# Gate weights of a retrieval layer: stored by 64 tokens instead of 32, with one-hot matrices built for 8 tokens at a time instead of 16

## The chip, the cores and the metric

The kernel runs on one core of a Trainium2 chip. The metric is the device time of one execution in microseconds. Before the change it is 2794.61 us, the median of 3 runs (2793.46 to 2800.45).

## The reference, cut to what matters

One layer of a trunk over 1024 tokens of width 1024, all in float32. An attention and a recurrent branch come first and play no part in the change. Then comes a retrieval layer (PEER) with 16384 experts; an expert is one neuron, a row of `expert_down` and a row of `expert_up`:

```python
v1, i1 = lax.top_k(s1, 16); v2, i2 = lax.top_k(s2, 16)      # per token, 8 heads
sc, ci = lax.top_k(v1[..., :, None] + v2[..., None, :], 16) # 16 of the 256 sums
eid = i1[ci // 16] * 128 + i2[ci % 16];  g = softmax(sc)    # 8 x 16 = 128 experts a token
act = gelu(einsum('thkd,td->thk', expert_down[eid], xb))
out = einsum('thk,thkd->td', g * act, expert_up[eid])
```

The output is the final RMSNorm of the residual plus this.

## The kernel before, in words

The 1024 tokens are 8 blocks of 128. The retrieval is done in two ways at once. For the first 3 blocks (NG) the kernel **gathers**: for each of 128 slots an indirect DMA on GpSimd's queue (L831) brings one 4 KB row for each of 128 tokens into one of 5 `row` buffers, and VectorE multiplies it (L848 for the down rows, L858 to add an up row into `accg`). That is 768 gathers. They are paced by `gather_steps(n)`, which is called from the loops of the other work; each VectorE step of a gather is pinned behind the VectorE instruction that was written just before it.

For the other 5 blocks (ND, 640 tokens, TD) the kernel is **dense**. The experts are 128 groups e of 128 neurons. For each e, `down_all` (L980) loads 512 KB of `down_t`, splits it into a high and a low part (ScalarE `dh`, VectorE `dl`) and runs 48 matmuls of 320 columns; the GELU of that is `ga`. It is weighted by a dense matrix of gates: for each token, a 128 x 128 matrix that is zero but in its 128 chosen places.

These gate matrices are made in the **one-hot stage** (L1078 to L1133). For TB tokens at a time, `one_hots` makes `o` (one-hot rows of both key indices, VectorE L1089, 3 buffers), `ov` (one of them times the gate's high and middle part, VectorE L1093, 2 buffers) and `oa` (times its low part, ScalarE, one instruction a token, L1100, 2 buffers). `weights` then runs 3 matmuls a token (L1113) into PSUM, 4 tokens to a bank, and ScalarE copies each bank into `st`, [128, 128 groups, TG tokens] (L1116, 2 buffers). When `st` has its TG tokens, two DMAs on ScalarE's queue store it to `gw_d` in HBM (L1118 the first 32 groups, L1119 the other 96). Each pass of the loop makes the one-hots of its own TB tokens, then, as its share comes due, a `down_all` whose result is kept in HBM (`act`; 40 of the 128 in this stage, one for each 16 tokens), then the matmuls of the TB tokens before, then its share of 168 gathers (none in the last 96 tokens). `turn` (L1126) transposes the top-k results of the last block at token 32.

In the **up stage** (L1138 on) `weigh(e)` reads, for every 4 groups e, `gw` (1280 KB, 2 buffers; L1151) from `gw_d`, takes `ga` from HBM (L1157) or from `down_all`, multiplies (L1162) and splits it into `w_h` and `w_l`. Then 15 matmuls of 512 columns for each e and half of the width add it to the output. `uraw` (L1189) are the rows of `expert_up`. Gathers run along here too. At the very end come those that are left and the final norm.

SyncE's queue (SP) issues `draw`, `uraw`, `acc`, `gw` and `ga` in order; ScalarE's queue issues `act` and the stores of `gw_d`; GpSimd's the gathers. The order of each engine's and queue's instructions is fixed at compile time by a planner, which takes the program's order as priority and moves an instruction up or down by its own estimate of when operands, buffers and transfers are ready; pinned instructions stay behind their predecessor. Memory on chip is a stack of pools: `sl`, `oh` and `stage` (which holds `st`) lie where `acc`, `up`, `wp` and `gp` (which holds `gw`) come later, so a new tile can wait for the last reader of an old one. The tile addresses of this kernel put the first `gw` buffer over the second `st` buffer.

The lines that make the stored layout and its read:

```python
gw_d = [dram.tile([TD // TG, P, n, TG], F32, name="gw_d") for n in (E_FIRST, NK - E_FIRST)]
gws[e // EQ] = gw = gp.tile([P, TD // TG, EQ * TG], F32, name="gw")
nc.sync.dma_start(gw, part[:, :, k:k + EQ, :].rearrange("a p e t -> p a (e t)"))
```

Of the kernel before, what the change touches and what calls it, by code (L numbers as in the profile page):

```python
# [43 lines left out]
EG = 8  # L44
EQ = 4
EARLY = 4
TG = 32
TB = 16
TI = 2

G_ATT, G_OUT, G_QRY, G_TOPK, G_OH = 45, 30, 30, 0, 168
# [1 line left out]
B_OUT, B_CHAIN, B_TURN, B_QRY, B_TOPK = 0, 3, 8, 8, 12  # L53
A_STEPS, A_AHEAD, A_FILL, LRU_AT, WO_AT = 3, 4, 0.5, 0.7, 50
E_QRY, E_TOPK, E_OH = 8, 20, 40
TURN5 = 2
OH_LAST = 96
NORM_IN = ((0,), (1,), (2, 3))
NORM_B = ((0, 1), (2, 3))
# [42 lines left out]
def trunk(  # L102
# [825 lines left out]
    with tc.tile_pool(name="op_d", bufs=1) as op, \  # L928
            tc.tile_pool(name="ps_od", bufs=3, space=PSUM) as ps_a:
        def turn(i, xt):  # L930
            for q in range(2):
                pt = ps_t.tile([P, 4, P], F32, name="pt")
                for j in range(4):
                    t = T.transpose(pt[:, j, :], xt[:, (4 * q + j) * P:(4 * q + j + 1) * P], ident)
                    if j == 0:
                        tc.keep_in_program_order(t)
                for j in range(4):
                    sl = (slice(None), 4 * q + j, slice(i * P, (i + 1) * P))
                    g2 = g2c[:, 4 * q + j:4 * q + j + 1]
                    A.activation(xH[sl], pt[:, j, :], AF.Copy, scale=g2)  # L940
                    V.scalar_tensor_tensor(xL[sl], pt[:, j, :], g2, xH[sl].bitcast(F32),
                                           op0=ALU.mult, op1=ALU.subtract)
# [31 lines left out]
    act_d = {}  # L974
    gw_d = [dram.tile([TD // TG, P, n, TG], F32, name="gw_d") for n in (E_FIRST, NK - E_FIRST)]

# [29 lines left out]
    with ExitStack() as ph:  # L1006
# [68 lines left out]
        V.tensor_copy(key_t, key_f[:, :, None].broadcast_to([P, P, TI]))  # L1075
        GB = TB // TI

        def one_hots(t0):  # L1078


            b, tt = divmod(t0, P)
            g0 = tt // TI

            def per_slot(t, n):
                return t[:, g0:g0 + GB, :, None, :].broadcast_to([P, GB, n, P, TI]).rearrange(
                    "p g n k i -> p (g n) k i")

            o = oh.tile([P, GB, 2, P, TI], BF, name="o21", bufs=3)
            V.tensor_tensor(o.rearrange("p g n k i -> p (g n) k i"),  # L1089
                            key_t[:, None, :, :].broadcast_to([P, GB * 2, P, TI]),  # L1090
                            per_slot(slot_k[b], 2), op=ALU.is_equal)
            ov = oh.tile([P, GB, 2, P, TI], BF, name="o1v", bufs=OB)
            V.tensor_tensor(ov.rearrange("p g n k i -> p g n (k i)"),  # L1093
                            o[:, :, 1:2, :, :].rearrange("p g n k i -> p g n (k i)").broadcast_to(
                                [P, GB, 2, P * TI]),
                            per_slot(slot_w[b], 2), op=ALU.mult)
            oa = oh.tile([P, GB, P, TI], BF, name="o1a", bufs=OB)
            for t in range(TB):
                g, j = divmod(t, TI)
                A.activation(oa[:, g, :, j], o[:, g, 1, :, j], AF.Copy,  # L1100
                             scale=slot_a[b][:, tt + t:tt + t + 1])
            return o, (ov[:, :, 0], ov[:, :, 1], oa)

        def weights(t0, o, parts):
            if t0 % TG == 0:
                sts[t0 // TG] = st_pool.tile([P, NK, TG], F32, name="st")
            st = sts[t0 // TG]
            for t4 in range(0, TB, 4):
                ps = ps_g.tile([P, 4, P], F32, name="pg")
                for t in range(t4, t4 + 4):  # L1110
                    g, j = divmod(t, TI)
                    for i, part in enumerate(parts):
                        T.matmul(ps[:, t - t4, :], o[:, g, 0, :, j], part[:, g, :, j],  # L1113
                                 start=i == 0, stop=i == 2)
                c = t0 % TG + t4
                A.copy(st[:, :, c:c + 4], ps.rearrange("p t i -> p i t"))  # L1116
            if (t0 + TB) % TG == 0:
                nc.scalar.dma_start(gw_d[0][t0 // TG], st[:, :E_FIRST, :])  # L1118
                nc.scalar.dma_start(gw_d[1][t0 // TG], st[:, E_FIRST:, :])  # L1119

        sts = {}
        last_five, last = last, None
        for t0 in range(0, TD, TB):
            now = one_hots(t0)
            if t0 == TURN5 * TB:
                turn(*last_five)  # L1126
# [153 lines left out]
```

## Time and profile before

| | us |
|---|---|
| median of 3 runs | 2794.61 |
| the profiled execution, its own time | 2791.39 |
| its span, first to last instruction | 2789.4 |
| TensorE (PE) busy | 2621.7 (94% of the span) |
| VectorE (DVE) busy | 2291.3 (82%) |
| ScalarE (ACT) busy | 1218.7 (44%) |
| GpSimd (POOL) busy | 1092.4 (39%) |

The profile counts 770 MB moved, 276 GB/s over the span. "PEclk" or "granted clock" is the share of TensorE's full clock (2.4 GHz) that it was given; 0.5 is 1.2 GHz. "DMA share" is the mean busy share of the 16 DMA engines. PEld is TensorE's weight load, SPq and ACTq are DMA issues of those queues. Of an instruction's row, the bracket says how long its engine stood idle before it and what ended that.

### The profile page before, as it was taken

Reading aid. Unit: us, or ns where it says so; the run is one execution under the profiler, and the core shown is the slowest. Engines: PE = TensorE matmul, PEld = TensorE weight load, DVE = VectorE, ACT = ScalarE, POOL = GpSimd, SP = SyncE. Lnnn points to the kernel's source line nnn. Section 1 sums busy time; section 2 is a strip of 40 time slices with the busy share of each in tenths; the row PEclk is TensorE's granted clock in tenths of the full one; section 3 lists DMA queues with packets and bytes.
Section 4 is the critical chain, followed back from the end, with each engine's and each line's share of the span. In section 5 each row is a group of like instructions: output and inputs, shape, how many; then the busy total and the mean of one; then the engine's idle time right before and its main releaser. Section 6 shows DMA issues by size and latency. Waiting matters only on the chain.

```text
span 2789.4 us, 43339 instructions
## 1 busy us (share of the span) xinstructions
PE 2621.7 (94%) x15489; PEld 2304.8 (83%) x15489; DVE 2291.3 (82%) x4838; ACT 1218.7 (44%) x2598; POOL 1092.4 (39%) x906
## 2 busy tenths in 40 slices
PE   7989988898999999999989999999999999999991
PEld 5765966647998999999978888888888888888871
DVE  7553879977999988989958888888888888888887
ACT  5652437824334667888833222222222222222220
POOL 2210035451111035444334445555455445545564
PEclk9999989999999999999999999999999999999996
DMA  6655489775544369999999999999999999999997
GB/s 199 144 139 174 119 196 235 227 276 182 181 142 132 111 234 336 347 344 340 331 364 336 340 325 345 348 323 340 338 339 336 320 344 340 339 327 341 333 316 257
DMA packets 316520, 770.05 MB, mean 276 GB/s; under 512 B 25632, under 2 KB 126000, under 8 KB 313744
## 3 DMA queue, kind: packets, MB, share of 16 engines
q0 software_dynamic: 136432, 425.67, 45.8%
q1 hardware_dynamic: 162768, 274.37, 29.2%
q10 hardware_dynamic: 17104, 67.25, 6.1%
q8 instruction: 121, 1.98, 0.3%
q14 instruction: 95, 0.78, 0.1%
HBM read 681.86 MB, written 85.33 MB: 275 GB/s over the span
## 4 chain that ended last, share of the span: by engine, by line
PE 75%; issue 9%; DMA 8%; DVE 4%; ACT 2%; POOL 2%; SPq 0%; DVEq 0%; POOLq 0%; ACTq 0%
PE pu L144 10%; PE pu L147 9%; PE pu L148 9%; PE pd L144 8%; PE pd L148 8%; PE pd L147 8%; PE pg L1113 4%; PE pa L144 2%; PE pa L148 2%; PE pa L147 2%; DMA row<-in_expert_up,eid 2%; PE pp L144 2%; PE pp L147 2%; PE pp L148 2%; DMA row<-in_expert_down,eid 2%
## 5 line engine op out<-in xcount | busy, mean ns | idle before, releaser
L831 POOL DMA_INDIRECT row<-in_expert_down,eid x384 | 507.8, 1322 | 660.0 <-DVE row L848 515.4
L831 POOL DMA_INDIRECT row<-in_expert_up,eid x384 | 505.0, 1315 | 587.2 <-DVE accg L858 403.5
L144 PE MATMUL pd<-xdH,dh 128*128 128x320 f32 x2048 | 639.8, 313 | 4.7 <-ACT dh L124 4.0
L148 PE MATMUL pd<-xdH,dl 128*128 128x320 f32 x2048 | 630.2, 312 | 13.4 <-DVE dl L125 13.3
L147 PE MATMUL pd<-xdL,dh 128*128 128x320 f32 x2048 | 635.2, 311 | 0.0
L858 DVE SCALAR_TENSOR_TENSOR accg<-row,wg,accg 128x1024 f32<-128x1024 f32 x384 | 491.4, 1280 | 23.8 <-DMA row<-in_expert_up,eid 21.3
L147 PE MATMUL pu<-ul,w_h 128*128 128x512 f32 x1280 | 501.9, 392 | 1.0 <-DVE ul L125 1.0
L148 PE MATMUL pu<-uh,w_l 128*128 128x512 f32 x1280 | 498.4, 391 | 0.0
L848 DVE SCALAR_TENSOR_TENSOR row<-row,x2g 128x1024 f32<-128x1024 f32 x384 | 462.5, 1219 | 23.2 <-DMA row<-in_expert_down,eid 22.5
L144 PE MATMUL pu<-uh,w_h 128*128 128x512 f32 x1280 | 393.9, 393 | 11.7 <-issue 5.2
L148 PEld LDWEIGHTS pd<-xdH,dl 128*128 128x128 f32 x2048 | 385.7, 189 | 21.6 <-DVE dl L125 15.5
L144 PEld LDWEIGHTS pd<-xdH,dh 128*128 128x128 f32 x2048 | 387.7, 189 | 12.9 <-ACT dh L124 4.3
L147 PEld LDWEIGHTS pd<-xdL,dh 128*128 128x128 f32 x2048 | 387.6, 189 | 7.5
L124 ACT CAST uh<-uraw 128x512 fp32r<-128x512 f32 x256 | 157.6, 620 | 472.3 <-PE pu L148 385.0
L144 PEld LDWEIGHTS pu<-uh,w_h 128*128 128x128 f32 x1280 | 236.7, 188 | 55.5 <-issue 7.3
L147 PEld LDWEIGHTS pu<-ul,w_h 128*128 128x128 f32 x1280 | 241.1, 188 | 48.7 <-DVE ul L125 1.8
L148 PEld LDWEIGHTS pu<-uh,w_l 128*128 128x128 f32 x1280 | 240.3, 188 | 48.4
L124 ACT CAST dh<-draw 128x512 fp32r<-128x512 f32 x256 | 158.0, 619 | 231.3 <-PE pd L147 225.8
L125 DVE TENSOR_TENSOR dl<-draw,dh 128x512 fp32r<-128x512 f32 x256 | 175.1, 687 | 74.5 <-ACT dh L124 74.0
L125 DVE TENSOR_TENSOR ul<-uraw,uh 128x512 fp32r<-128x512 f32 x256 | 175.5, 687 | 65.3 <-ACT uh L124 64.9
L124 ACT CAST w_h<-ga 128x640 fp32r<-128x640 f32 x128 | 93.2, 729 | 245.2 <-PE pu L147 148.8
L1100 ACT ACTIVATE o1a<-o,slot_a 128x128 bf16<-128x128 bf16 x640 | 194.7, 430 | 0.6 <-issue 0.3
(265 smaller groups left out, 4089.5 us busy)
## 6 DMA issues: line engine op xcount, KB each, us to landing
draw<-in_down_t SPq DMA_DIRECT2D x128, 512.0 KB, 7.0
uraw<-in_up_h SPq DMA_DIRECT2D x128, 512.0 KB, 6.8
gw<-gw_d SPq DMA_DIRECT2D x32, 1280.0 KB, 16.4
gw_d<-st ACTq DMA_DIRECT2D x20, 1536.0 KB, 11.5
act<-ga ACTq DMA_DIRECT2D x70, 320.0 KB, 4.8
ga<-act SPq DMA_DIRECT2D x70, 320.0 KB, 9.8
wraw<-in_w_query SPq DMA_DIRECT2D x64, 256.0 KB, 3.1
gw_d<-st ACTq DMA_DIRECT2D x20, 512.0 KB, 7.4
```

The lines of the kernel that those rows point to most:

```text
L124: A.copy(hi, src)
L125: (eng or V).tensor_sub(lo, src, hi.bitcast(F32))
L144: t = T.matmul(ps, wh, mh, start=first, stop=False)
L147: T.matmul(ps, wh, ml, start=False, stop=False)
L148: T.matmul(ps, wl, mh, start=False, stop=last)
L831: nc.gpsimd.indirect_dma_start(out=r, out_offset=None, in_=table, in_offset=bass.IndirectOffsetOnAxis(ap=eids[tb][:, s:s + 1], axis=0))
L848: tc.keep_in_program_order(V.scalar_tensor_tensor(r, r, 1.0, x2, op0=ALU.mult, op1=ALU.mult, accum_out=act[:, s:s + 1]))
L858: tc.keep_in_program_order(V.scalar_tensor_tensor(acc, r, w[:, s:s + 1], acc, op0=ALU.mult, op1=ALU.add))
L1100: A.activation(oa[:, g, :, j], o[:, g, 1, :, j], AF.Copy, scale=slot_a[b][:, tt + t:tt + t + 1])
L1113: T.matmul(ps[:, t - t4, :], o[:, g, 0, :, j], part[:, g, :, j], start=i == 0, stop=i == 2)
```

## The change

Three constants. TG is the number of tokens that one `st` tile and one slab of `gw_d` hold; TB the number of tokens for which one call of `one_hots` and of `weights` works; TURN5 counts in units of TB and keeps `turn` at token 32.

```diff
-TG = 32
-TB = 16
+TG = 64
+TB = 8
 TI = 2
...
-TURN5 = 2
+TURN5 = 4
```

By the code above this means: `one_hots` is called 80 times instead of 40, each VectorE instruction in it has half the elements; the buffers of `o`, `ov` and `oa` keep their number and have half the size; a `down_all` comes in every second pass of the loop; a call of `gather_steps` hands out half as many gathers, twice as often; `st` is twice as large and is stored 10 times, with twice the bytes each time; a `gw` read has the same bytes in contiguous runs of 4 x 64 x 4 bytes = 1 KB instead of 512 B.

## Rows read from the trace of the kernel before

**Rows 1.** Stretches of the span: us, busy of each engine (instructions), clock, DMA share, GB/s

```profile
1300.00:1406.00 106.00, 106.00 (x1071) 104.88 (x1070) 92.97 (x72) 93.35 (x252) 41.24 (x31) 1.00 0.92 341
1406.00:1427.00 21.00, 20.67 (x141) 20.40 (x140) 11.41 (x12) 5.91 (x13) 7.07 (x6) 1.00 1.02 418
1427.00:1460.00 33.00, 21.77 (x101) 19.56 (x102) 15.42 (x17) 6.05 (x11) 7.39 (x7) 0.79 0.98 344
1500.00:1600.00 100.00, 100.00 (x528) 88.77 (x527) 80.96 (x133) 28.64 (x49) 40.99 (x35) 1.00 0.94 335
2733.00:2789.00 56.00, 0.17 (x1) 0.00 (x0) 42.34 (x101) 1.87 (x4) 25.34 (x20) 0.53 0.72 257
```

**Rows 2.** Waits of TensorE, 956 to 1406 us: us in total, times, longest

```profile
PE pd L148 <- DVE dl L125: 5.4, 2, 5.1
```

**Rows 3.** Groups by shape, 956 to 1406 us: busy us, mean ns | idle before

```profile
L1093 DVE TENSOR_TENSOR o1v<-o,slot_w 128x4096 bf16<-128x4096 bf16 x38 | 87.0, 2289 | 6.3 <-PE pg L1113 6.2
L1089 DVE TENSOR_TENSOR o<-key_t,slot_k 128x4096 bf16<-128x4096 bf16 x37 | 84.5, 2284 | 3.1 <-PE pg L1113 3.1
L665 DVE TENSOR_TENSOR wt<-ge,dx 128x2048 bf16<-128x2048 bf16 x5 | 6.1, 1218 | 0.1
```

**Rows 4.** VectorE in order of time, one pass of the one-hot loop: start, us

```profile
1382.99 2.30 DVE L1093 TENSOR_TENSOR o1v<-o,slot_w 128x4096 bf16<-128x4096 bf16 x1 [0.29 <-PE pg L1113]
1385.21 2.28 DVE L1089 TENSOR_TENSOR o<-key_t,slot_k 128x4096 bf16<-128x4096 bf16 x1
1387.42 1.27 DVE L858 SCALAR_TENSOR_TENSOR accg<-row,wg,accg 128x1024 f32<-128x1024 f32 x1
1388.87 0.69 DVE L125 TENSOR_TENSOR dl<-draw,dh 128x512 fp32r<-128x512 f32 x1 [0.18 <-ACT dh L124]
...
1392.86 2.30 DVE L1093 TENSOR_TENSOR o1v<-o,slot_w 128x4096 bf16<-128x4096 bf16 x1 [0.29 <-PE pg L1113]
```

**Rows 5.** The chain of waits in order of time: the gate matmuls of two passes: start, us

```profile
1350.67 2.77 PE pg L1113 x48
1360.53 2.77 PE pg L1113 x48
```

**Rows 6.** DMA issues, whole span: count, KB each, median us to landing

```profile
draw<-in_down_t SPq DMA_DIRECT2D x128, 512.0 KB, 7.0
gw<-gw_d SPq DMA_DIRECT2D x32, 1280.0 KB, 16.4
gw_d<-st ACTq DMA_DIRECT2D x20, 1536.0 KB, 11.5
```

**Rows 7.** Issue queues of ScalarE and SyncE at the handover to the up stage: start, us

```profile
1406.51 0.76 ACTq L1119 DMA_DIRECT2D gw_d<-st  x1
...
1427.27 14.21 SPq L1151 DMA_DIRECT2D gw<-gw_d  x2
1441.57 6.34 SPq L985 DMA_DIRECT2D draw<-in_down_t  x1
1447.95 0.91 SPq L1157 DMA_DIRECT2D ga<-act  x2
```

**Rows 8.** VectorE at the handover: start, us, [idle before]

```profile
1447.33 0.83 DVE L1162 TENSOR_TENSOR ga<-ga,gw 128x640 f32<-128x640 f32 x1 [4.65 <-DMA gw<-gw_d]
1455.07 0.83 DVE L1162 TENSOR_TENSOR ga<-ga,gw 128x640 f32<-128x640 f32 x1 [4.10 <-DMA ga<-act]
1458.34 0.82 DVE L1162 TENSOR_TENSOR ga<-ga,gw 128x640 f32<-128x640 f32 x1
```

**Rows 9.** Waits from 1406 us to the end: us in total, times, longest

```profile
DVE ga L1162 <- DMA ga<-act: 53.5, 13, 5.9
DVE accg L858 <- DMA row<-in_expert_up,eid: 18.7, 24, 2.6
```

**Rows 10.** Gathers issued after 2733 us, and VectorE's last of them

```profile
L831 POOL DMA_INDIRECT row<-in_expert_up,eid x20: 937/1208/1918, 2732.1 to 2765.0; - x20
2769.42 2.69 DVE L858 SCALAR_TENSOR_TENSOR accg<-row,wg,accg 128x1024 f32<-128x1024 f32 x2 [0.74 <-DMA row<-in_expert_up,eid]
```

## The prediction

> **What bounds the kernel now.** I read the stretches of the span first [rows 1]. From 1300 to 1406 us, at the end of the one-hot stage, TensorE is busy the whole time at full clock, while VectorE is busy 88% (92.97 of 106), ScalarE 88% and the DMA engines 92%. So TensorE sets the pace there, with three resources close behind it. In the list of its waits from 956 to 1406 us TensorE has one entry, 5.4 us [rows 2]: the one-hots never keep it waiting. From 1500 us TensorE is again busy without a break (100.00 of 100), and what it does there the change does not touch. Two stretches are not TensorE's. The first is the handover, 1406 to 1460 us. There the DMA engines are full (418 GB/s, share 1.02), and between 1427 and 1460 TensorE runs 101 matmuls in 33 us at a clock of 0.79 [rows 1]; at the 528 in 100 us of the up stage these are 19.1 us of work, so 13.9 us are lost. The second is the end: after 2733 us TensorE does nothing (0.17 us busy) and GpSimd still issues 20 gathers, from 2732.1 to 2765.0 us; VectorE ends the last at 2772.1 [rows 1, 10]. So each gather that is left at the end costs (2772.1 - 2733.1) / 20 = 1.95 us, and the final norm follows.
>
> The time therefore has three parts that the change could move: whether TensorE stays fed in the one-hot stage, what is lost at the handover, and how many gathers are left at the end.
>
> **Part 1: one-hots of 8 tokens.** VectorE runs 80 more instructions (40 more of `o`, 40 more of `ov`), each with 2048 elements instead of 4096. A 4096-element instruction takes 2289 ns, a 2048-element one of the same kind 1218 ns [rows 3]: two halves cost 2 x 1218 - 2289 = 147 ns more than the whole. Back to back a little of this overlaps: `ov` started at 1382.99 us with a length of 2.30, and the next began at 1385.21, 0.08 earlier than its end [rows 4]. So an added instruction costs 67 to 147 ns, and the 80 cost 5.4 to 11.8 us, 0.13 to 0.29 us for each 16 tokens. A pass for 16 tokens lasts 1392.86 - 1382.99 = 9.87 us, and VectorE idles 0.29 + 0.18 = 0.47 us of it [rows 4]. The cost fits into this, so I count it at nothing on the path. If the cover is gone, VectorE drops gathers and not matmuls, which is a rival below. ScalarE gets no more instructions: `oa` is one for each token and the copies to `st` one for each 4 tokens, as before; it issues 20 store DMAs less.
>
> The buffers are the other side of it. `o`, `ov` and `oa` held 48, 32 and 32 tokens, and now hold 24, 16 and 16. Two calls of `weights` come between two `down_all`, so TensorE eats 16 tokens in one burst, which is all that `ov` holds, and VectorE must refill both buffers while the 48 matmuls of a `down_all` run. Already now `ov` starts 0.29 us after TensorE frees its buffer [rows 4]; one-hot instructions waited 6.2 + 3.1 us for TensorE in all [rows 3], and that stays a wait of VectorE for TensorE as long as the refill is in time. The refill is two `ov` and at most two `o`, 4 x 1.22 = 4.9 us by the 2048-element row. The window is the pass less the burst. The bursts are 2.77 us long and begin every 1360.53 - 1350.67 = 9.86 us [rows 5], which leaves 7.1 us; the 4.9 and a gather or two fit into that, and the rest of the pass's gathers beside the burst. I take 0. Bounds: a gain is excluded below -5.4 us, since TensorE waits only that long in the stage [rows 2]; above, 40 passes that each slip by the 0.29 us are +12 us.
>
> **Part 2: the store.** One slab is now 4 MB, with 10 of them for 20; bytes and packets per byte of the stores' long runs are no more than before. Only the last one matters, since it goes out when TensorE has ended the last tokens (the last issue is at 1406.51 [rows 7]). The first `gw` tile lies over the `st` buffer that is stored last, so its load waits for this store. Now the larger DMA of a pair takes 11.5 us [rows 6], landed by 1418, and the load is issued at 1427.27 [rows 7]: the wait is over before. With twice the bytes it takes 23 us by that row, to 1429.5, which delays the load by 2 us; at the 418 GB/s of the full engines [rows 1] the 2.1 MB more are 5 us. I take +3. Bounds: 0 to +12 (the whole doubling comes late).
>
> **Part 3: the read.** A `gw` read has 1280 packets of 1 KB for 2560 of 512 B. In the queue rows, two `gw` issues together hold SP for 14.21 us, the `draw` behind them another 6.34, and only then, at 1447.95, the `ga` loads go out [rows 7]. The first multiply has its gates at 1447.33, the second waits for `ga` until 1455.07, the third is at 1458.34 [rows 8]. I read the 14 us as a queue that is full of packets; with half of them the `ga` loads go out earlier. Then the second multiply follows the first as the third follows the second: 7.74 - 3.27 = 4.5 us less. I take -4. Bounds: 0 to -14, the whole loss of the handover.
>
> For the other 30 loads I count nothing. TensorE does not wait there, and VectorE's waits for transfers after 1406 us are small beside 1380 us: 53.5 us for `ga`, 18.7 us for the up rows [rows 9]. Nor do the rows show that the short runs are slow: 512 KB of `draw` take 7.0 us and 1280 KB of `gw` 16.4 us [rows 6], which is 2.34 times for 2.5 times the bytes.
>
> The Trainium skill, "DMA: Bandwidth & Descriptors", section Specifications, says the same, that 512 B are enough for the full rate of a transfer. Its section "Why small descriptors are slow (HBM only)" speaks against it: each packet costs about 3 cycles beside one for each 32 bytes, by which a 512 B run needs 19 cycles and half of a 1 KB run 17.5, 8% less. By the landing times above this trace agrees with the first; the 8% is small enough to hide in it.
>
> **The sum.** 0 + 3 - 4 = -1 us. The profiled execution took 2791.39 us, 3.2 us (0.12%) under the median of 2794.61, so the forecast is 2790 for it and 2793.6 on the median's footing; I say 2793. A measurement of this kernel can tell about 0.3%, 8.4 us, from no change.
>
> **The rivals.** *Fewer gathers left.* In the one-hot stage, without `gw`, the engines move 341 GB/s, in the up stage, with it, 335 [rows 1]. That both come out alike, while 418 are possible, looks as if the planner paces the gathers by what it thinks a transfer costs, and puts their steps so late on VectorE that 20 are left. If it (and the chip) charges the 512 B runs extra, the halved count lets gathers move forward. All 20 are 20 x 0.524 = 10.5 MB, 31 us at 335 GB/s; the 32 `gw` loads are 41.9 MB, 125 us. So a quarter of their time must be saved to lose the whole tail, which gives 20 x 1.95 = 39 us, 2755; an eighth gives 2774. Against it: the landing times per byte, and that gathers hardly wait for their rows.
>
> By the 8% of that page of the Trainium skill, 10 us of transfer time would be saved, 6 gathers, 12 us: 2782.
>
> *More gathers left (slower).* Place: VectorE in the one-hot stage, which now fits three gathers into each pass (one and two more in the gap of [rows 4]) with 0.47 us to spare. If the 80 instructions cost their full 11.8 us there and are not covered, 11.8 / 1.27 = 9 gathers [rows 4] are pushed back; if the up stage carries the lag on to the end, they cost 9 x 1.95 = 18 us: 2812. It decides the sign from 5 gathers on. For it: VectorE is the fullest engine after TensorE. Against: the idle rest is larger than the cost.
>
> *The handover gets longer (slower).* The store doubles, holds the first `gw` for 12 us, and SP's queue behind it: 2806 if nothing is won by Part 3.
>
> *The change does nothing of what it says.* If the run on the HBM side stayed 512 B, Part 3 falls away: 2797, no change either.
>
> **How the numbers follow.** No change (with the last rival): 0.40. Fewer gathers left, or a handover cured by more than 8 us: 0.35. More gathers left: 0.15; a longer handover or a starved TensorE: 0.10. So faster 0.35, same 0.40, slower 0.25. The likeliest case's own range is 2785 to 2802. The range is 2757 to 2814: it takes in nearly all of the first rival and the 18 us of the second.
>
> **What would show it.** Part 1: TensorE's waits between 956 and 1406 us stay under 10 us and the stage's last matmul for the gates ends within 3 us of 1406; `o` and `ov` at about 1218 ns, 80 each. Part 2: the larger store lands in about 23 us and the first `gw` is issued at 1427 to 1432. Part 3: the second `gw` issue no longer holds SP for 14 us, and 1280 packets less a load; `gw`'s landing stays near 16 us. The end: 18 to 22 gathers after TensorE's last matmul. The prediction is wrong if that count falls under 15 or rises over 25, or if TensorE waits for `o1v` or `o` in the one-hot stage by more than 10 us.

## The result and the profile after

The changed kernel took 2816.78 us (median of 4 runs, 2809.15 to 2818.96) against 2794.53 for the kernel before beside it: a ratio of 1.007, interval 1.0047 to 1.0094. It is slower by 0.7%, outside the predicted range. The profiled execution took 2818.96 us with a span of 2817.0, so 27.6 us of span have to be found. These lines of its page are the engines and the DMA queues; the columns of the latter are packets, MB and share of the 16 engines.

```profile
PE 2647.3 (94%) x15489; PEld 2321.4 (82%) x15489; DVE 2298.2 (82%) x4918; ACT 1218.1 (43%) x2598; POOL 1106.6 (39%) x906
DMA packets 272680, 770.05 MB, mean 273 GB/s; under 512 B 25312, under 2 KB 84720, under 8 KB 269904
q10 hardware_dynamic: 14224, 67.25, 6.0%
```

VectorE has 2298.2 us of work in 4918 instructions for 2291.3 in 4838, so the 80 added ones cost 6.9 us, within the 5.4 to 11.8 of the prediction. The stretches, in the columns of [rows 1], show where the time is:

```profile
1100.00:1200.00 100.00, 99.53 (x965) 97.71 (x963) 94.68 (x99) 86.33 (x241) 62.78 (x32) 1.00 0.94 352
1200.00:1300.00 100.00, 88.38 (x819) 85.24 (x816) 84.54 (x107) 79.59 (x226) 39.60 (x26) 0.92 0.84 316
1300.00:1406.00 106.00, 98.60 (x858) 94.49 (x858) 89.30 (x86) 70.48 (x194) 51.97 (x34) 0.97 0.86 329
1406.00:1455.00 49.00, 48.15 (x472) 47.27 (x471) 44.04 (x44) 41.64 (x116) 26.57 (x14) 1.00 0.83 302
1455.00:1476.00 21.00, 15.25 (x100) 14.72 (x99) 8.63 (x9) 4.57 (x9) 7.02 (x7) 0.96 0.99 395
1476.00:1509.00 33.00, 25.71 (x132) 23.13 (x131) 14.51 (x16) 5.52 (x10) 4.80 (x6) 0.86 1.04 396
1550.00:1650.00 100.00, 100.00 (x522) 88.29 (x521) 81.05 (x133) 26.90 (x47) 45.20 (x37) 1.00 0.94 342
2795.00:2817.00 22.00, 0.38 (x2) 0.00 (x0) 16.68 (x82) 1.87 (x4) 0.00 (x0) 0.58 0.45 177
```

From 1300 to 1406 us TensorE now ran 858 matmuls where it ran 1071 [rows 1]; from 1200 to 1300 it was busy 88.38 of 100 us, and its granted clock was 0.92 in the mean: it fell to the lower of its two levels, 1.2 GHz, where TensorE had kept waiting (just before the first fall, from 1208.0 to 1218.2 us, it was busy for 6.36). The last gate matmul (L1113) starts at 1454.7 us for 1405.3 before: +49.4. From there to TensorE's last matmul it is 1340.3 us for 1327.5: +12.8. And from there to the end it is 22.0 us for 56.6: -34.6, since no gather is issued any more where there were 20 [rows 10]. The sum is +27.6. So the one-hot stage lost the time, and the end gave back two thirds of it. TensorE's waits from 956 to 1455 us, one row before [rows 2], are now these (total, times, longest) and two smaller ones, 2.6 us together:

```profile
PE pg L1113 <- DVE o1v L1093: 8.6, 8, 2.4
PE pd L148 <- DVE dl L125: 7.8, 6, 3.5
PE ptk L1043 <- DVE five L620: 6.6, 1, 6.6
PE pg L1113 <- ACT st L1116: 6.3, 5, 2.1
```

They name the one-hots and other work of VectorE. Its groups by shape in the same stretch (as [rows 3]):

```profile
L858 DVE SCALAR_TENSOR_TENSOR accg<-row,wg,accg 128x1024 f32<-128x1024 f32 x82 | 105.0, 1281 | 19.1 <-DMA row<-in_expert_up,eid 18.7
L1093 DVE TENSOR_TENSOR o1v<-o,slot_w 128x2048 bf16<-128x2048 bf16 x77 | 93.8, 1220 | 14.9 <-PE pg L1113 14.7
L1089 DVE TENSOR_TENSOR o<-key_t,slot_k 128x2048 bf16<-128x2048 bf16 x76 | 91.6, 1219 | 0.0
L848 DVE SCALAR_TENSOR_TENSOR row<-row,x2g 128x1024 f32<-128x1024 f32 x50 | 59.6, 1219 | 9.4 <-DMA row<-in_expert_down,eid 9.4
```

The one-hots take 1219 ns, as forecast. VectorE stood still for gathered rows for 28.1 us. In the kernel before, its only such wait from 956 to 1406 us was

```profile
DVE row L848 <- DMA row<-in_expert_down,eid: 6.6, 3, 2.8
```

It also made 14 gather steps more in its longer stretch, 132 for 118; what those cost is taken up at the end. One wait for a row, in order of time, with what stands behind it:

```profile
1233.58 1.22 DVE L1089 TENSOR_TENSOR o<-key_t,slot_k 128x2048 bf16<-128x2048 bf16 x1
1240.85 1.23 DVE L848 SCALAR_TENSOR_TENSOR row<-row,x2g 128x1024 f32<-128x1024 f32 x1 [6.06 <-DMA row<-in_expert_down,eid]
1242.00 0.08 DVE L848 DVE_READ_ACCUMULATOR row<-row,x2g 128x1 f32 x1
1242.00 0.69 DVE L125 TENSOR_TENSOR dl<-draw,dh 128x512 fp32r<-128x512 f32 x1
1242.61 1.22 DVE L1093 TENSOR_TENSOR o1v<-o,slot_w 128x2048 bf16<-128x2048 bf16 x1
```

In VectorE's order `dl`, which TensorE's next matmuls need, and `o1v` stood behind a row that had not landed. ScalarE had issued a store at 1225 us; that the store made the row late is for the experiments to show. The DMA queues in the 20 us behind a store: queue (q10 is ScalarE's, q0 the gathers'), packets, MB, share of the 16 engines, and the gathers issued with their median time to landing. First the kernel before, behind a store of 2 MB (from 1196.1 us):

```profile
q10 hardware_dynamic: 697, 3.02, 38.5%
q0 software_dynamic: 730, 2.65, 34.9%
row<-in_expert_down,eid POOLq DMA_INDIRECT x6, 8.4
```

The changed kernel, behind 4 MB (from 1224.9 us):

```profile
q10 hardware_dynamic: 576, 4.85, 59.3%
q0 software_dynamic: 682, 2.53, 33.6%
row<-in_expert_down,eid POOLq DMA_INDIRECT x6, 16.2
```

The gathers land in 16.2 us instead of 8.4, behind fewer packets of ScalarE's queue but larger ones: 8.4 KB on the mean (`act` included) for 4.3. Behind the other stores of the stage the median is 14.3 to 17.7 us.

At the handover the issues went nearly as forecast, but the work behind them did not. The median landing of the larger store is 17.7 us and of `gw` 14.3:

```profile
gw<-gw_d SPq DMA_DIRECT2D x32, 1280.0 KB, 14.3
gw_d<-st ACTq DMA_DIRECT2D x10, 3072.0 KB, 17.7
...
gw_d<-st ACTq DMA_DIRECT2D x10, 1024.0 KB, 6.5
```

SyncE's queue there (start, us; a row of several issues includes the waits between them):

```profile
1445.31 30.95 SPq L985 DMA_DIRECT2D draw<-in_down_t  x4
1476.43 5.68 SPq L1151 DMA_DIRECT2D gw<-gw_d  x2
```

The first `gw` goes out 21.7 us after the last gate matmul (22.0 before, [rows 7]), and two of them hold the queue for 5.68 us instead of 14.21. Two issues of `uraw` behind them hold it for another 9.78 us, and the `ga` loads go out 17.0 us behind the first `gw` for 20.7 [rows 7]. VectorE's first multiplies by the gates, and the four gather steps that stood before the second:

```profile
1493.31 0.82 DVE L1162 TENSOR_TENSOR ga<-ga,gw 128x640 f32<-128x640 f32 x1 [2.20 <-DMA gw<-gw_d]
...
1506.93 5.24 DVE L858 SCALAR_TENSOR_TENSOR accg<-row,wg,accg 128x1024 f32<-128x1024 f32 x4
1512.09 1.55 DVE L1162 TENSOR_TENSOR ga<-ga,gw 128x640 f32<-128x640 f32 x2
```

### The profile page after: what moved, and what is told of

It is laid out like the page before. It is cut to its first block, busy times and chain, and to the rows that moved or that the text cites. A ratio compares the mean times of both kernels' runs of the same rounds, so it can differ in the third digit from the quotient of the medians.

```text
span 2817.0 us, 43385 instructions
## 1 busy us (share of the span) xinstructions
PE 2647.3 (94%) x15489; PEld 2321.4 (82%) x15489; DVE 2298.2 (82%) x4918; ACT 1218.1 (43%) x2598; POOL 1106.6 (39%) x906
## 4 chain that ended last, share of the span: by engine, by line
PE 66%; issue 12%; DMA 11%; DVE 5%; POOL 4%; ACT 2%; SPq 0%; DVEq 0%; POOLq 0%; ACTq 0%
PE pu L144 10%; PE pu L147 10%; PE pu L148 10%; PE pd L148 6%; PE pd L144 6%; PE pd L147 6%; DMA row<-in_expert_up,eid 6%; POOL row L831 4%; PE pa L144 2%; PE pa L148 2%; PE pa L147 2%; PE pp L144 2%; PE pp L147 2%; PE pp L148 2%; PE pa L796 1%
## 5 line engine op out<-in xcount | busy, mean ns | idle before, releaser
L831 POOL DMA_INDIRECT row<-in_expert_down,eid x384 | 499.9, 1302 | 734.4 <-DVE row L848 589.6
L831 POOL DMA_INDIRECT row<-in_expert_up,eid x384 | 526.7, 1372 | 566.9 <-DVE accg L858 367.2
L848 DVE SCALAR_TENSOR_TENSOR row<-row,x2g 128x1024 f32<-128x1024 f32 x384 | 461.8, 1219 | 30.4 <-DMA row<-in_expert_down,eid 30.1
L1100 ACT ACTIVATE o1a<-o,slot_a 128x128 bf16<-128x128 bf16 x640 | 199.9, 433 | 17.7 <-DVE o L1089 17.2
## 6 DMA issues: line engine op xcount, KB each, us to landing
gw<-gw_d SPq DMA_DIRECT2D x32, 1280.0 KB, 14.3
gw_d<-st ACTq DMA_DIRECT2D x10, 3072.0 KB, 17.7
```

The lines of the kernel that those rows point to most:

```text
L831: nc.gpsimd.indirect_dma_start(out=r, out_offset=None, in_=table, in_offset=bass.IndirectOffsetOnAxis(ap=eids[tb][:, s:s + 1], axis=0))
L848: tc.keep_in_program_order(V.scalar_tensor_tensor(r, r, 1.0, x2, op0=ALU.mult, op1=ALU.mult, accum_out=act[:, s:s + 1]))
L1100: A.activation(oa[:, g, :, j], o[:, g, 1, :, j], AF.Copy, scale=slot_a[b][:, tt + t:tt + t + 1])
```

## The experiments

All ratios are to the kernel before, run beside each.

**Each half of the change alone.** First the one-hots of 8 with slabs of 32 tokens (the changed kernel with `TG = 32`).

> The changed kernel with 32 tokens to a slab again (TG = 32): one-hots for 8 tokens alone. In the profile of the changed kernel the last gate matmul starts at 1454.7 us, against 1405.3 before; that is the number to watch. Theory A (large stores): a 4 MB store makes the gathered rows land late, VectorE waits for them in its order, and TensorE runs out of one-hots; with 2 MB stores the last gate matmul comes back to 1405 to 1420 us, VectorE waits under 3 us for rows between 1060 and 1400, and the time is 2790 to 2802. Theory B (thin buffers): 16 tokens of one-hots in stock are too few with any store; the last gate matmul stays at 1440 to 1455 and the time at 2808 to 2820.

2793.31 us, ratio 0.9993 (0.9978 to 1.0008); last gate matmul at 1408.3 us, and TensorE's waits from 956 to 1408 us are

```profile
PE pd L144 <- ACT ga L997: 0.5, 1, 0.5
PE pg L1113 <- ACT st L1116: 0.3, 1, 0.3
```

VectorE's row waits in 940 to 1400 us are 2.1 us. So the added instructions and the thinner buffers cost nothing by themselves. It takes the slab of 64 to make the loss.

**The store in eight pieces.** The changed kernel with

```diff
+                for k in range(0, NK, 16):
+                    part, k0 = (gw_d[0], k) if k < E_FIRST else (gw_d[1], k - E_FIRST)
+                    pieces.append((part[t0 // TG][:, k0:k0 + 16, :], st[:, k:k + 16, :]))
+            for _ in range(len(pieces) if t0 + TB == TD else min(1, len(pieces))):
+                nc.scalar.dma_start(*pieces.pop(0))
```

> The changed kernel, with each 4 MB slab stored in 8 pieces of 512 KB, one after each pass of 8 tokens, instead of two DMAs at once; nothing else. Theory A (large stores): no burst, so the rows come in time, the last gate matmul is at 1405 to 1420 us, and the time is 2775 to 2800, with the 1 KB reads kept. Theory B (thin buffers): still 1440 to 1455, and 2808 to 2820.

2831.92 us, ratio 1.013 (1.0113 to 1.0147): worse, and the last gate matmul is at 1474.8 us, outside both expectations. But it was not the experiment that I had meant. The planner, which may move an instruction up, had moved the pieces together. ScalarE's stream, start and length, behind one slab:

```profile
1196.30 1.19 ACTq L1122 DMA_DIRECT2D gw_d<-st  x1
1197.56 4.04 ACTq L1122 DMA_DIRECT2D gw_d<-st  x3
1201.65 0.44 ACT L997 ACTIVATE ga<-pd 128x320 f32<-128x320 f32 x1 [3.67 <-issue]
```

Issues one behind another held ScalarE for 3.67 us here, and TensorE's waits for `st` grew from 6.3 to 25.6 us (956 to 1460). The rows, however, came nearly in time: VectorE waited 4.4 us for them in 940 to 1400 us (23.8 in the changed kernel), although nearly as much left at once. The pieces have runs of 4 KB in HBM. That was the first sign that it is not the amount alone.

**A third `o1v` buffer** (`bufs=OB + 1`).

> The changed kernel with a third buffer for ov (the two weighted one-hots), 24 tokens in stock instead of 16; o and oa as they are. Theory B (thin buffers): at least half of the 49 us come back, last gate matmul at 1405 to 1430, time 2790 to 2805. Theory A (large stores): VectorE still waits 1 to 6 us for rows some 15 us after each store, and since o (3) and oa (2) stay as short, less than a third comes back: 1438 to 1455, time 2805 to 2820.

2804.72 us, ratio 1.0029 (1.0017 to 1.0042), below the changed kernel's interval. VectorE's row waits were as long as before (24.1 us in 940 to 1400). The last gate matmul stayed at 1453.4 us (1454.7), where theory B had it at 1405 to 1430. So the third buffer did not give the stage back, and the thin buffers are not the cause. The time is at the lower edge of theory A's range. Of the 7.9 us between the two profiled executions 6.6 lie behind the stage (1355.7 us for 1362.3), and what made them is not shown.

**No gathers in the stage** (`G_OH = 0`; the 168 come in the up stage and at the end, so the total says nothing).

> The changed kernel with the 168 gathers of the one-hot stage handed out in the up stage instead. Read for the one-hot stage alone: the time as a whole must grow, since 168 gathers more go to the end at some 2 us each as far as the up stage can't take them. If VectorE's waits for rows are the trigger (theory A), the last gate matmul comes to under 1415 us with no wait of TensorE for one-hots over 2 us in all. If the buffers are too thin for the burst of 16 tokens by themselves (theory B), it stays over 1435.

The stretch from 1100 to 1300 us, in the columns of [rows 1]:

```profile
1100.00:1300.00 200.00, 200.00 (x1961) 197.95 (x1959) 123.03 (x123) 174.39 (x488) 0.00 (x0) 1.00 0.53 195
```

TensorE never waits, and the last gate matmul is at 1397.5 us. With the same slabs, stores and buffers the loss is gone, so it takes the gathers. That it goes through their late rows this run does not show by itself, since VectorE also has less to do without them (123 of 200 us) and the DMA engines too (0.53).

**4 MB at once, in slabs of 32.** One-hots of 8, `TG = 32`, four `st` buffers, two slabs stored together:

```diff
+            if (t0 + TB) % (2 * TG) == 0:
+                for a in (t0 // TG - 1, t0 // TG):
+                    tc.keep_in_program_order(nc.scalar.dma_start(gw_d[0][a], sts[a][:, :E_FIRST, :]))
+                    tc.keep_in_program_order(nc.scalar.dma_start(gw_d[1][a], sts[a][:, E_FIRST:, :]))
```

> Slabs of 32 tokens and one-hots for 8 (as in the run that took the time of before), four st buffers of 16 KB instead of two, and the stores of two slabs held back, by a pin to the program's order, until the second is full: 4 MB leave at once every 64 tokens, as in the changed kernel, but in the layout of before (512 B runs in the reads). Theory A, the rows come late because 4 MB of store stand in the DMA engines at once: as in the changed kernel, 2805 to 2830 us, last gate matmul after 1430 us, VectorE's waits for gathered rows 15 to 50 us in the stage and within 25 us of a store. Theory C, the cause is the slab of 64 in itself (its layout, or the order that the planner makes of it) and not how much leaves at once: within 0.3% of before, last gate matmul before 1412 us, row waits under 5 us.

2801.08 us, ratio 1.0024 (1.0008 to 1.004), last gate matmul at 1428.3 us, row waits of 13.0 us in 940 to 1400 us. The time is within theory C's range; the row waits and the last gate matmul lie between the two. With runs of 12 KB the amount at once costs some 8 us against the slabs of 32 alone, a third of the loss, with the pins and the two added buffers counted in. Behind such a store gathers landed in 15.3 us (from 1176 us), nearly as late as in the changed kernel.

**The spread, pinned.** As the eight pieces above, but two a pass and each pinned with `keep_in_program_order`.

> The changed kernel with each slab of 64 stored in 8 pieces of 512 KB, two behind the copies of each of the four passes that follow, pinned to that place: in the earlier run without a pin the planner had moved the pieces up, and six to eight of them were issued one straight after another. Theory A: with 1 MB at a time the rows are in time, 2785 to 2805 us, last gate matmul before 1420 us, row waits under 10 us and no wait of ScalarE's copies for a free st. Theory C: as the changed kernel, 2810 to 2825 us, last gate matmul after 1440 us. If ScalarE is held by the issues themselves (as in the unpinned run, up to 4.7 us for three), TensorE's waits for st stay near 25 us and the time near 2830 us.

2787.04 us, ratio 0.9975 (0.9961 to 0.9989): faster than the kernel before. Last gate matmul at 1411.8 us, 11 gathers left behind TensorE's last matmul. VectorE's only row wait in 940 to 1400 us is

```profile
DVE row L848 <- DMA row<-in_expert_down,eid: 1.8, 1, 1.8
```

This cures the loss, but it changes two things: what leaves at once, and the run in HBM, now 16 groups x 64 tokens x 4 B = 4 KB instead of 8 and 24.

**A quarter of the bytes.** The changed kernel without the 3 MB store (the other 96 groups of gates are not stored; the up stage reads the first 32 again).

> The changed kernel without the larger of the two stores: only the first 32 groups of gates are stored (1 MB for each slab instead of 4 MB), and the up stage reads those again in place of the other 96. The reads and all other work stay. Theory A: the stage is as before or shorter, last gate matmul before 1412 us, VectorE's row waits under 5 us in 1040 to 1400 us, time 2765 to 2797 us. Theory C or the order of the instructions alone: last gate matmul after 1440 us, time 2805 to 2825 us.

2773.56 us, ratio 0.9929 (0.9908 to 0.9951), but the last gate matmul is at 1428.8 us: between the two expectations. The stage made 253 gathers by then, for 228 in the kernel before and 245 in the changed one, 40 of them between 1150 and 1250 us, where TensorE was busy 86.03 of 100. VectorE's row waits there are 7.2 us (940 to 1400), above theory A's 5, and TensorE waited 14.7 us for `o1v` (956 to 1460). So the stage is longer than before even without the large store. That it is so by the gathers made earlier, which are then not left at the end, is a reading and not shown.

**The packets alone.** The same two stores at the same places, with runs of 4 KB by the layout of `gw_d`:

```diff
-    gw_d = [dram.tile([TD // TG, P, n, TG], F32, name="gw_d") for n in (E_FIRST, NK - E_FIRST)]
+    gw_d = [dram.tile([TD // TG, n // 16, P, 16, TG], F32, name="gw_d") for n in (E_FIRST, NK - E_FIRST)]
...
+                    nc.scalar.dma_start(part[t0 // TG].rearrange("q p n t -> p q n t"),
+                                        s16.rearrange("p (q n) t -> p q n t", n=16))
```

> The changed kernel with its two stores at the same places and of the same size (1 MB and 3 MB at once), but gw_d laid out so that each partition's run in HBM is 16 groups long: 4 KB pieces instead of 8 and 24 KB. In the one-hot stage every engine has the same instructions in the same order as in the changed kernel. After a store of the changed kernel, its queue took 57.8% of the DMA engines with 531 packets in 20 us, and gathers landed in 18.0 us. Theory D, a gathered row (4 KB packets) waits its turn behind store packets of 24 KB: with packets of its own size it gets its share, rows land in about 12 us after a store, VectorE's row waits fall from 24 us to under 10 us in 940 to 1400 us, last gate matmul before 1425 us, time 2785 to 2805 us. Theory A, it is the 4 MB at once, whatever the packets: last gate matmul 1440 to 1460 us, 2808 to 2825 us. Theory O, it is the order of the instructions: the same as A.

2790.71 us, ratio 0.9983 (0.9969 to 0.9996): 26 us less than the changed kernel, with the order of every engine in the stage unchanged. It is within theory D's range. VectorE's row waits in 940 to 1400 us, 14.0 and 9.8 us in the changed kernel, are

```profile
DVE accg L858 <- DMA row<-in_expert_up,eid: 2.8, 4, 0.8
DVE row L848 <- DMA row<-in_expert_down,eid: 2.4, 3, 1.2
```

The queues in the 20 us behind the store that answers to the one shown above (from 1217 us):

```profile
q10 hardware_dynamic: 1002, 4.04, 49.6%
q0 software_dynamic: 725, 2.65, 37.2%
```

ScalarE's queue has 1002 packets now for 576, and a smaller share; the gathers have a larger one. When they land can't be read from this trace. The last gate matmul moved from 1454.7 to 1430.7 us, not to the 1425 that I had written. From 956 us to there TensorE does the same 4210 matmuls in both kernels; first the changed one, then the layout run, in the columns of [rows 1]:

```profile
956.00:1455.00 499.00, 470.17 (x4210) 457.69 (x4211) 433.39 (x592) 372.22 (x1001) 224.04 (x130) 0.97 0.80 294
956.00:1431.00 475.00, 459.49 (x4210) 448.09 (x4211) 432.26 (x572) 371.31 (x1000) 214.63 (x131) 1.00 0.84 309
```

Of the 24.0 us, 13.3 are less waiting (28.8 to 15.5 us not busy). The other 10.7 are the same matmuls in less busy time, at a granted clock of 1.00 for 0.97: with the late rows TensorE lost clock as well as time in waiting.

The layout also moves the runs in HBM. Against that as the cause speak the two spreads above: they wrote runs of 4 KB into the unchanged layout, and VectorE's row waits were 4.4 and 1.8 us.

**Large packets, spread.** The pinned spread cut by partitions (32 partitions with all groups at a time), so that the runs stay 8 and 24 KB.

> The changed kernel with the spread of the run that was faster than before (a quarter of a slab behind each of the four passes that follow, pinned), but cut by partitions: 32 partitions with all 128 groups at a time, so that the packets stay 8 and 24 KB. Theory A (what leaves at once decides): as the spread with 4 KB packets, 2780 to 2795 us, last gate matmul before 1420 us. Theory D (packet size decides): rows late, last gate matmul after 1430 us, 2800 to 2825 us; with both at work something between.

2809.42 us, ratio 1.0076 (1.0052 to 1.0101), row waits of 14.0 us in 940 to 1400 us, last gate matmul at 1427.5 us: the time and the rows of theory D, but a stage between the two theories and no longer than the layout run's. TensorE's largest wait there (940 to 1400, total, times, longest) is not for `o1v`:

```profile
PE pg L1113 <- ACT st L1116: 10.5, 8, 2.1
```

Together with three other runs:

| us, median | runs of 8 and 24 KB | runs of 4 KB |
|---|---|---|
| 4 MB at once | 2816.78 | 2790.71 |
| 1 MB behind each of four passes | 2809.42 | 2787.04 |

By the medians the run length makes 22 to 26 us and the spread 4 to 7; by the ratios, each to the kernel before beside it, the spread can't be told from nothing (1.007 and 1.0076, 0.9983 and 0.9975). Only the upper row is a clean test of the runs. In the lower one the cut by partitions brings more: TensorE waited 2.3 us for `o1v` and 10.5 for `st`, ScalarE's store issues took 0.687 us in the median for 0.499 in the pinned spread, and of the 25.8 us between the two profiled executions the stage makes 15.7. What part of the 22 us is the runs' stays open.

**The spread in slabs of 32** (one-hots of 8, four pieces of 512 KB, 4 KB runs, pinned).

> Slabs of 32 tokens and one-hots for 8, each slab stored in four pieces of 512 KB (4 KB packets), two behind each of the two passes that follow, pinned: the spread without the slab of 64, reads in 512 B runs. If the gain of the spread with slabs of 64 over the kernel before (0.25%) came from the spread, this has it too: 2780 to 2792 us. If it came from the 1 KB reads, this is as before, 2790 to 2798 us.

2791.18 us, ratio 0.9985 (0.997 to 1.0). It lies in both of the expected ranges, which overlap; what the reads of 1 KB are worth can't be told from it (0.9975 with them, the intervals overlap).

**The spread with a third buffer**, and **20 gathers more in the stage** (`G_OH = 188` on top of it).

> The spread with slabs of 64 (eight pieces of 512 KB, pinned) and a third buffer for the one-hots times gates. In the spread run TensorE still waited 8.1 us for those in the stage. Theory B (the stock of 16 tokens is thin also without late rows): 3 to 8 us faster than the spread run, 2779 to 2784 us, last gate matmul 1403 to 1408 us. If the stock was thin only where rows came late: the same time as the spread run within 3 us.

> The spread with a third buffer (slabs of 64, eight pinned pieces) and 188 instead of 168 gathers given out in the stage, 20 fewer later. Over the runs so far, the time from the last gate matmul to the end has fallen by 1.3 to 1.6 us for each gather that was made before that matmul, beyond the 228 of before. Theory E (the stage has room for them, now that rows come in time): last gate matmul within 10 us of the spread run with a third buffer (1419 us), 15 to 20 more gathers by then, time 2762 to 2778 us. Theory F (VectorE, 93% busy in 1050 to 1420 us there, has none: 20 gathers are 25 us of it): the stage grows by 20 to 30 us and gives back what the end saves, 2780 to 2792 us.

2784.09 us, ratio 0.9962 (0.9949 to 0.9975), and 2788.84 us, ratio 0.9977 (0.9965 to 0.9989). The first is the best version here, 0.4% under the kernel before; that it is better than the spread alone is not resolved, and where rows are in time the third buffer gave 3 us, not the 12 of above. Its last gate matmul, at 1419.1 us, was later than the spread's 1411.8, against theory B. The 8.1 us that the expectation names count idle weight loads too; TensorE's matmuls had waited 3.1 us. In the second only 3 more gathers were made by the last gate matmul (241 for 238), which came at 1427.1 us for 1419.1. The stage grew by 8 us, not by 20 to 30, and the time is in theory F's range: the stage gave back what the end saved, with few gathers moved. Whether that is for want of room on VectorE is not shown.

## Why the prediction was wrong

The step that failed is in Part 2: "bytes and packets per byte of the stores' long runs are no more than before. Only the last one matters". I took the size of a packet as harmless as long as there were no more of them, and priced only the last store, at the handover. All ten stand beside gathers, and the runs grew from 4 and 12 to 8 and 24 KB. The layout run shows what those of 8 and 24 KB cost against 4 KB: 24.0 us of the stage and 26 us of the time, with not an instruction moved in the stage. The trace of before had a warning, though not of the packets: behind a store of 2 MB its gathers landed in 8.4 us, and behind the last one, beside more traffic, in 12.0. I looked at VectorE's row waits only after 1406 us, where all stores but the last are over [rows 9]; in the stage they were 6.6 us.

How the larger packets delay a row is not measured by itself. In the 20 us behind a store the gathers' queue and ScalarE's moved 682 and 576 packets with the large runs, 730 and 697 in the kernel before, and 725 and 1002 with runs of 4 KB. By the Trainium skill, "DMA: Bandwidth & Descriptors", section "Queues, rings and completion order", an engine serves its queues in turn and changes only at the end of a packet. These counts do not settle whether that is the cause: the two queues are not one to one in the last pair, and whether the page's packet, which it gives as several descriptors, is the one counted here no run shows.

*Part 1* held where it stood alone (the run with one-hots of 8: 0.9993). Its "I take 0" for the buffers assumed that VectorE's gathers cost their 1.27 us and no wait; with late rows TensorE waited, and a third buffer did not shorten the stage. The criterion that I had set, 10 us for `o1v`, was not reached (8.6): TensorE's waits came under several names, 31.9 us in all. What showed it was the end of the stage, forecast within 3 us of 1406 and 49.4 us later.

*Part 2, the handover:* the store landed in 17.7 us, not 23, and the first `gw` was issued no later than before. The +3 was too much.

*Part 3:* the reads have 1 KB runs (40960 packets fewer on SyncE's queue), two issues hold it 5.68 us instead of 14.21, the `ga` loads went out 3.7 us earlier behind the first `gw`, and a load lands in 14.3 us for 16.4. But the second multiply, with four gather steps before it, came 18.8 us behind the first instead of 7.7 [rows 8], and TensorE was busy 41.0 us of the 54 us of the handover for 42.4 [rows 1]: the gain of 4 us did not come. Its count that the reads matter nowhere else is neither shown nor refuted.

*The rivals.* "More gathers left" had the sign and, with 2812, nearly the size, and named VectorE in the one-hot stage as the place. That was luck: the gathers left went from 20 to 0, not to 29 (under 15 was a sign of being wrong), and the loss that the layout run gives back was VectorE's standing still, not its work. The first rival's tail of fewer gathers did come, -34.6 us, and so hid more than half of what the stage lost. It came with an order of the planner that puts more of them into the stage, 245 for 228 by the last gate matmul. Over the runs that make all of the work, the time behind the last gate matmul was shorter by 0.6 to 2.0 us for each gather made before it beyond the 228 of the kernel before (up to 249 in the run with a third buffer alone; 246 in the layout run), a wider range than the 1.3 to 1.6 that I wrote before the last run. Of the stage's +49.4 us the layout run, which has the same order, keeps 25.4; what makes them is not shown. All this compares runs with different orders, so the price of one gather is not shown by itself. The +12.8 us of the up stage is not traced to a cause; the layout run has +8.9 of it.

## What to carry to other kernels

Before a transfer is made larger, look at the packet it is cut into and at what shares the DMA engines with it, not only at its own landing time and its end: small gathers that stand in an engine's fixed order landed twice as late behind 4 MB in runs of 8 and 24 KB as behind 2 MB in runs of 4 and 12. Choose the HBM layout so that the packets of a bulk store are small beside such a transfer; here runs of 4 KB, the size of a gathered row, took one more dimension in a tile's shape, and they were worth 0.9%. Where the limit lies was not tried: runs of 12 KB cost nothing with 2 MB at once (0.9993) and a little with 4 (1.0024). A spread written in the program is none until the order of the queue shows it, so read the issue times before judging it.

## What was not expected of the hardware

DMA issues on ScalarE's queue are not free when they follow each other: the smaller store of each pair in the changed kernel took 0.33 us to issue and the larger 0.44 to 1.67, but three in a row 4.04 us, with ScalarE's own work held behind them for 3.67. And the large packets cost no throughput that these rows show: in the 20 us behind the first four stores the engines moved 7.92 to 8.13 MB with them and 7.94 to 8.24 MB with packets of 4 KB. The rate does not show the loss; the landings of the gathers and VectorE's waits do.
